# Both attention layers follow an explicit plan of steps

## The chip, the cores and the metric

The kernel runs on one core of a Trainium2 chip. Measured is the device time of one execution in microseconds. Times of the kernel before: 1265.6, 1262.97 and 1261.54 us, median 1262.97.

## The reference

Two transformer layers over T = 512 tokens with D = 1024, in float32:

```
for layer in range(2):
    h = rmsnorm(x, attn_norm[layer])
    if layer == 0:
        fq, fk, fv, ff, dq, ckv, dkr, iq, ik, iw = split(h @ w_in_even)
        fox  = softmax(fq fk' / 8 + c_q - c_k, causal) fv          # 8 heads, c = cumsum(log_sigmoid(ff + b))
        sel  = top_128(sum_h iw_h relu(iq_h ik'), causal)          # per query, 4 index heads
        dsa  = softmax over sel of (dq . [rope key | ckv w_uk]) ; times ckv w_uv   # 8 heads
        x    = x + concat(fox, dsa) @ w_out_even
    else:
        mq, mk, mv = split(h @ w_in_odd)                           # 16 heads, rope on mq and mk
        x    = x + softmax(mq mk' / 8, causal) mv @ w_out_odd
    x = x + conv_glu_ffn(rmsnorm(x, ffn_norm[layer]))
return rmsnorm(x, final_norm)
```

The blocked attention of layer 1 selects one earlier block of 256 keys beside the own block; with 512 tokens these are all keys up to the query, so it is causal attention.

## The kernel before

Everything is held with features on the partitions (xT, 8 tiles of 128 x 512). Each float32 operand is split into a high and a low part, and a product is three matmuls (mm3, L157 to 161). A projection (proj, L163) reads a weight chunk of 128 x 1024: SP loads it into raw_*, ACT copies the high part wh_*, POOL in the attentions of layer 0 (DVE elsewhere) subtracts the low part wl_*. Three buffers each are there for raw, wh and wl, so the SP instruction that loads a chunk waits until the chunk three places earlier has been split. A projection has 24 matmuls of 512 columns; a value group (v_group, L388) has 96 of 256 columns over two chunks and gives the values of two pairs of heads.

The heads are taken in pairs: f0 to f3 and d0 to d3 in layer 0, m0 to m7 in layer 1. A pair's queries are split into h and l and rearranged by three copies of 64 x 512 within SBUF (stack_q, L246: two into the tile a, one into l); its keys by six (stack_k, L255). These moves are issued by SP, on the queue that carries the weights. soft (L332) makes the scores s_* of one head in four blocks of queries on PE, their reductions and masks on DVE (prt_*), the exponentials on ACT, the scaling by POOL. mix (L356) transposes the probabilities on PE (t_*), splits them with ACT and DVE (pt_*, p), and multiplies with the values (o_*). For the d heads a mask tmask comes from index_scores (L608: matmuls ix, then ACT and DVE or POOL) and select (L625), 16 rounds of two DVE instructions for each of three blocks of queries. The values of d come from dv (two PSUM tiles in the pool mm, which has three buffers), split by ACT and DVE.

The program is written in an order that serves as a priority: the framework's scheduler lists the instructions of each engine ahead of time, and each engine then runs its list in order. In the attentions heads() (L527) sets this order: it takes a list of work with due pairs, emits the scores of a head, then a share of the work due by the next pair (the projections of the next pair, selection, output projections), then the mix of the head before. So each pair's keys and queries are projected one pair ahead. In layer 1 the factor 1/rms (rstd_main) and the scaled rope tables are made within the first value group (moba_scale, L741).

Of the kernel before, what the change touches and what calls it, by code (L numbers as in the profile page):

```python
# [71 lines left out]
def hybrid_kernel(ctx: ExitStack, tc: tile.TileContext, xT_d, pos_d, const_d, vec_d, w_d, out_d, idx):  # L72
    nc = tc.nc
    V, A, G, PE = nc.vector, nc.scalar, nc.gpsimd, nc.tensor
# [13 lines left out]
    def tmp(name):  # L88
        return tp.tile([P, T], F32, tag="tmp", name=name, bufs=N_TMP)
# [266 lines left out]
    def mix(nm, e, probs, v, hv, y):  # L356

        par = head_no[0] % 2
        head_no[0] += 1
        rs = (LO, HI)[e]  # L360
        o = ps("O", f"o_{nm}")
        pt = [(big(f"pt_{nm}_{j}h"), big(f"pt_{nm}_{j}l")) for j in range(2)] + [tuple(p3[par])]
        for b in range(3):
            t = ps("T", f"t_{nm}_{b}")
            if b < 2:
                blocks = [(b, i) for i in range(b, NB)]
                segs = [(0, P * len(blocks), 0)]
            else:
                blocks = [(2, 2), (2, 3), (3, 3)]
                segs = [(0, 256, 0), (256, 384, 384)]  # L370
            for n, (j, i) in enumerate(blocks):
                PE.transpose(t[:, n * P:n * P + P], probs[i][:, j * P:j * P + P], ident)  # L372
            ph, pl = pt[b]
            for s0, s1, d0 in segs:
                d1 = d0 + s1 - s0
                split(ph[:, d0:d1], pl[:, d0:d1], t[:, s0:s1])
        for j in range(NB):
            ph, pl = pt[min(j, 2)]
            c0, w, o0 = ((0, T, 0), (0, 384, P), (0, 256, 256), (256, 256, 256))[j]
            vj = v[:, j, hv].rearrange("p s c -> p (s c)")  # L380
            PE.matmul(o[:, o0:o0 + w], vj, ph[:, c0:c0 + w], start=j == 0, stop=False)  # L381
            PE.matmul(o[:, o0:o0 + w], vj, pl[:, c0:c0 + w], start=False, stop=j == NB - 1)
        A.copy(y[rs], o[HI])
        V.tensor_tensor(y[rs], y[rs], o[LO], op=OP.add)
# [139 lines left out]
                done(2 * p + e, Q[1])  # L524
        last(Q[1])

    def heads(pairs, work):  # L527


        work = list(work)  # L530
        prev = None

        def finish(pr):
            p, e, probs = pr
            c = pairs[p]
            mix(f"{c['nm']}{e}", e, probs, values[c["v"]], c["hv"] + e, c["y"])
            if e == 1:
                c["out"].append(halves(c["y"], f"o_{c['nm']}", c.get("lo", V)))

        for p, c in enumerate(pairs):  # L540
            while work and work[0][0] <= p:
# [125 lines left out]
    def fox(p):  # L667
        def vals():
            values["f", p // 2] = v_group(f"fv{p // 2}_")

        def qs():
            c["q"] = stack_q(scaled(proj(f"fq{p}"), f"fq{p}"), f"fq{p}")

        def ks():
            c["k"] = stack_k(scaled(proj(f"fk{p}"), f"fk{p}"), f"fk{p}", G)

        c = {"nm": f"f{p}", "v": ("f", p // 2), "hv": 2 * (p % 2), "bias": causal, "out": fo, "lo": G,
             "decay": [(selr[:, P + h:P + h + 1], ck) for h in (2 * p, 2 * p + 1)]}
        return c, ([vals] if p % 2 == 0 else []) + [ks, qs]

    def dsa(p):
        def vals():
            uh, ul = ukv[0]
            g = p // 2
            vg = vtile(f"dv{g}")
            for b in range(2):
                o = ps("mm", f"mm_dv{g}_{b}", (P, 2, 256))
                for bb in range(2):
                    s = slice((2 * b + bb) * P, (2 * b + bb + 1) * P)
                    ws = slice(512 + 256 * g, 768 + 256 * g)  # L690
# [19 lines left out]
        return c, [ks, qs] + ([vals] if p % 2 == 0 else [])  # L710

    pairs, work = [], []
    for n in range(8):
        c, w = (fox if n < 4 else dsa)(n % 4)
        pairs.append(c)
        if n == 0:
            w = [x for i, f in enumerate(w) for x in (f, lambda i=i: index_scores(i + 1))]
        elif n == 2:
            w.append(lambda: select(1, range(16)))
        elif n > 2 and n < 5:  # L720
            w[1:1] = [lambda n=n: select(n - 1, range(8))]
            w.append(lambda n=n: select(n - 1, range(8, 16)))
        work += [(n, f) for f in w]
        if n == 7:
            work.append((7, lambda: out_proj("oe0_", fo, part=[0])))
    work += [(8, lambda m=m: out_proj("oe0_", fo, part=[m])) for m in range(1, 4)]
    heads(pairs, work)
# [11 lines left out]


    def moba_scale():  # L741
        rstd_main(accs[2], "n2")
        rope_scaled()

    mo = ([], [])

    def moba(p):
        def vals():
            values["m", p // 2] = v_group(f"mv{p // 2}_", moba_scale if p == 0 else None)

# [7 lines left out]
        return c, ([vals] if p % 2 == 0 else []) + [ks, qs]

    pairs, work = [], []  # L760
    for n in range(8):
        c, w = moba(n)
        pairs.append(c)
        work += [(n, f) for f in w]
        if n == 7:
            work.append((7, lambda: out_proj("oo0_", mo[0], part=[0])))
    work += [(8, lambda m=m: out_proj("oo0_", mo[0], part=[m])) for m in range(1, 4)]
    heads(pairs, work)
# [156 lines left out]
```

## Time and profile before

| | |
|---|---|
| median of three runs | 1262.97 us |
| profiled execution | 1261.51 us, span 1259.7 us |
| mean granted clock of TensorE | 0.993 |
| attention of layer 0 (about) | 57 to 290 us of the span |
| attention of layer 1 (about) | 636 to 905 us of the span |

Busy time is the sum of an engine's instructions; matmuls overlap each other in it. A line of the timeline has a start, a busy time, the instruction with output and inputs, and in brackets the idle time ahead of it with what ended it. Granted clock 1.00 is full speed of TensorE.

### The profile page before, as it was taken

How to read it: one execution, taken by the hardware profiler on the slowest of the kernel's cores; microseconds unless marked ns; L12 is line 12 of the kernel's file. 1: busy time of each engine (PE TensorE's matmuls, PEld its weight loads, DVE VectorE, ACT ScalarE, POOL GpSimd, SP SyncE). 2: the span in 40 equal slices, each digit the busy share in tenths (PEclk: the TensorE clock that was granted, in tenths of full speed). 3: DMA queues.
4: the chain of work that ended last, by engine and by line, in shares of the span. 5: the costliest groups of instructions: out<-in, count | busy, mean ns of one | idle time of the engine just before them, and what ended most of it. 6: DMA issues, size and time to landing. Idle time of an engine off the chain costs nothing.

```text
span 1259.7 us, 16807 instructions
## 1 busy us (share of the span) xinstructions
PE 1220.4 (97%) x5996; PEld 1018.3 (81%) x5996; DVE 810.9 (64%) x1489; ACT 557.4 (44%) x969; POOL 357.7 (28%) x394
## 2 busy tenths in 40 slices
PE   6889999999999999999999999999999999999997
PEld 4768778778888888888887888888888888888887
DVE  7889988675654555544666778787655555444555
ACT  5564667653332333333445556555433333332334
POOL 3665557542111111111213223332222111111110
PEclk9989999999999999999999999999999999999999
DMA  5333444222333322323325434331233332333321
GB/s 194 101 92 111 128 99 128 63 80 89 101 100 100 98 90 93 96 93 100 103 96 142 113 100 123 105 109 67 84 93 108 100 100 92 94 100 101 96 88 67
DMA packets 57379, 127.24 MB, mean 101 GB/s; under 512 B 7584, under 2 KB 21024, under 8 KB 57296
## 3 DMA queue, kind: packets, MB, share of 16 engines
q1 hardware_dynamic: 56368, 124.81, 33.2%
q10 hardware_dynamic: 864, 1.17, 0.3%
q8 instruction: 47, 0.77, 0.2%
q14 instruction: 36, 0.29, 0.1%
q0 software_dynamic: 64, 0.20, 0.0%
HBM read 104.13 MB, written 2.10 MB: 84 GB/s over the span
## 4 chain that ended last, share of the span: by engine, by line
PE 79%; DVE 10%; issue 5%; ACT 3%; DMA 2%; POOL 1%; POOLq 0%; ACTq 0%; DVEq 0%; SPq 0%
PE mm_g L160 6%; PE mm_g L161 6%; PE mm_g L159 6%; PE mm_u L161 6%; PE mm_u L159 6%; PE mm_u L160 6%; PE mm_d L161 6%; PE mm_d L160 6%; PE mm_d L159 6%; DVE tmask L630 2%; DVE m L629 1%; DMA mq_l<-mq_h 1%; PE t_m L372 1%; PE o_m L381 1%; PE mm_mk L160 1%
## 5 line engine op out<-in xcount | busy, mean ns | idle before, releaser
L434 POOL TENSOR_TENSOR cv<-cv,gs 128x512 f32<-128x512 f32 x44 | 57.1, 1298 | 546.2 <-ACT gs L433 546.2
L159 PE MATMUL mm_d<-a_h,wh_d 128*128 128x512 f32 (+1 forms) x384 | 142.8, 372 | 0.0
L160 PE MATMUL mm_d<-a_l,wh_d 128*128 128x512 f32 (+1 forms) x384 | 142.6, 371 | 0.0
L161 PE MATMUL mm_d<-a_h,wl_d 128*128 128x512 f32 (+1 forms) x384 | 142.6, 371 | 0.0
L503 DVE TENSOR_TENSOR us<-mm_u,cv 128x512 f32<-128x512 f32 x44 | 30.4, 692 | 168.1 <-PE mm_u L161 132.7
L160 PE MATMUL mm_g<-xl,wh_g 128*128 128x512 f32 x352 | 137.2, 390 | 0.4 <-DVE xl L175 0.4
L159 PE MATMUL mm_u<-xh,wh_u 128*128 128x512 f32 x352 | 137.3, 390 | 0.0
L161 PE MATMUL mm_u<-xh,wl_u 128*128 128x512 f32 x352 | 137.0, 389 | 0.0
L160 PE MATMUL mm_u<-xl,wh_u 128*128 128x512 f32 x352 | 137.0, 389 | 0.0
L161 PE MATMUL mm_g<-xh,wl_g 128*128 128x512 f32 x352 | 137.0, 389 | 0.0
L159 PE MATMUL mm_g<-xh,wh_g 128*128 128x512 f32 x352 | 137.0, 389 | 0.0
L148 ACT CAST wh_g<-raw_g 128x1024 fp32r<-128x1024 f32 x44 | 46.3, 1052 | 143.1 <-PE mm_g L160 141.6
L500 DVE TENSOR_TENSOR gs<-mm_g,RB 128x512 f32<-128x512 f32 x44 | 30.4, 691 | 118.2 <-PE mm_g L161 115.7
L128 ACT CAST wh_d<-raw_d 128x1024 fp32r<-128x1024 f32 x45 | 47.4, 1054 | 123.7 <-PE mm_u L160 103.4
L160 PEld LDWEIGHTS mm_d<-a_l,wh_d 128*128 128x128 f32 x384 | 72.3, 188 | 12.5
L159 PEld LDWEIGHTS mm_d<-a_h,wh_d 128*128 128x128 f32 x384 | 72.3, 188 | 12.5
L161 PEld LDWEIGHTS mm_d<-a_h,wl_d 128*128 128x128 f32 x384 | 72.3, 188 | 12.4
L160 PEld LDWEIGHTS mm_g<-xl,wh_g 128*128 128x128 f32 x352 | 66.1, 188 | 14.8 <-DVE xl L175 1.1
L161 PEld LDWEIGHTS mm_u<-xh,wl_u 128*128 128x128 f32 x352 | 66.1, 188 | 13.8
L159 PEld LDWEIGHTS mm_g<-xh,wh_g 128*128 128x128 f32 x352 | 66.1, 188 | 13.7
L161 PEld LDWEIGHTS mm_g<-xh,wl_g 128*128 128x128 f32 x352 | 66.1, 188 | 13.7
L160 PEld LDWEIGHTS mm_u<-xl,wh_u 128*128 128x128 f32 x352 | 66.1, 188 | 13.6
(778 smaller groups left out, 3072.4 us busy)
## 6 DMA issues: line engine op xcount, KB each, us to landing
raw_g<-in_w SPq DMA_DIRECT2D x44, 512.0 KB, 3.5
raw_u<-in_w SPq DMA_DIRECT2D x44, 512.0 KB, 3.6
raw_d<-in_w SPq DMA_DIRECT2D x41, 256.0 KB, 2.9
raw_d<-in_w SPq DMA_DIRECT2D x29, 192.0 KB, 2.6
raw_d<-in_w SPq DMA_DIRECT2D x34, 128.0 KB, 2.4
raw_oe<-in_w SPq DMA_DIRECT2D x8, 512.0 KB, 4.0
raw_mv<-in_w SPq DMA_DIRECT2D x8, 512.0 KB, 3.5
raw_mk<-in_w SPq DMA_DIRECT2D x8, 512.0 KB, 4.0
```

Of the source, the lines that this page charges most:

```text
L128: A.copy(dst_h, src)
L148: A.copy(wh, raw)
L159: PE.matmul(out, ah, bh, start=first, stop=False)
L160: PE.matmul(out, ah, bl, start=False, stop=False)
L161: PE.matmul(out, al, bh, start=False, stop=last)
L372: PE.transpose(t[:, n * P:n * P + P], probs[i][:, j * P:j * P + P], ident)
L381: PE.matmul(o[:, o0:o0 + w], vj, ph[:, c0:c0 + w], start=j == 0, stop=False)
L434: G.tensor_tensor(cv, cv, gs, op=OP.mult)
L500: V.tensor_tensor(gs, og, RB, op=OP.mult)
L503: V.tensor_tensor(us, ou, cv, op=OP.mult)
L629: V.max(m8, sc)
L630: V.match_replace(sc, m8, sc, -3e38)
```

## The change

heads() goes, and attention() takes its place: it reads a string of steps and emits them as they stand. s is the scores of a head (pair, head), m its mix, k, q and v the projections of a pair (v of a value group), i the index scores of a block, x a quarter of a selection (block, quarter), o a part of the output projection of the finished half. The old order of layer 0 began v0 i1 k0 i2 q0 i3 s00 k1 s01 q1 m00 s10 v2 k2 m01 s11 q2, with all rounds of select(1) behind q2. What a step computes is unchanged; moba_scale is called by whichever projection of layer 1 comes first.

```
+PLAN0 = (
+    "v0 i1 k0 i3 i2 q0 s00 x10 v2 k1 s01 q1 m00 s10 k2 s11 q2 x11 x12 m01 x13 x20 s20 m10 k3 s21 x21 m11 "
+    "x22 x23 x30 q3 s30 m20 k4 x31 q4 s31 v4 x32 x33 m21 m30 s40 k5 m31 s41 q5 m40 s50 k6 q6 m41 s51 q7 "
+    "m50 s60 v6 m51 o0 m60 k7 s61 s70 m61 m70 s71 o1 o2 m71 o3 "
+)
+PLAN1 = (
+    "q1 q0 k0 k1 v0 s00 s01 s10 k2 s11 m00 k3 q4 q2 m01 v2 k4 q3 m10 m11 s20 s21 v4 s30 m20 m21 s31 k5 "
+    "m30 k7 s40 m31 s41 o0 q5 v6 m40 s50 k6 m41 s51 q6 s60 m50 m51 o1 q7 s61 s70 m60 o2 m61 m70 s71 m71 "
+    "o3 "
+)
-    def heads(pairs, work):
...
-            for e in range(2):
-                probs = soft(...)
-                n = len([1 for w in work if w[0] <= p + 1])
-                for _ in range((n + 1 - e) // (2 - e)):
-                    work.pop(0)[1]()
-                if prev is not None:
-                    finish(prev)
-                prev = (p, e, probs)
...
+    def attention(pairs, plan, pieces):
+        probs = {}
+        for step in plan.split():
+            kind, n = step[0], step[1:]
+            if kind == "s":
+                c, e = pairs[int(n[0])], int(n[1])
+                if e == 0:
+                    c["y"] = tmp(f"y_{c['nm']}")
+                probs[n] = soft(...)
+            elif kind == "m":
+                c, e = pairs[int(n[0])], int(n[1])
+                mix(f"{c['nm']}{e}", e, probs.pop(n), values[c["v"]], c["hv"] + e, c["y"])
+                if e == 1:
+                    c["out"].append(halves(c["y"], f"o_{c['nm']}", c.get("lo", V)))
+            else:
+                pieces[kind](int(n))
...
+    attend([fox(p) for p in range(4)] + [dsa(p) for p in range(4)], PLAN0,
+           i=index_scores, x=lambda n: select(n // 10, range(n % 10 * 4, n % 10 * 4 + 4)),
+           o=lambda m: out_proj("oe0_", fo, part=[m]))
...
     def moba_scale():
-        rstd_main(accs[2], "n2")
-        rope_scaled()
+        if 2 in accs:
+            rstd_main(accs.pop(2), "n2")
+            rope_scaled()
...
+        def qs():
+            o = proj(f"mq{p}")
+            moba_scale()
+            c["q"] = stack_q(rope(o, f"mq{p}"), f"mq{p}")
...
+    attend([moba(p) for p in range(8)], PLAN1, o=lambda m: out_proj("oo0_", mo[0], part=[m]))
```

In the listings below, helper lines of the new kernel stand 13 further down; raw_* are weight loads of 512 KB, 64x512 are moves, the numbers in names are buffers'. First, the SP queue around the moves of fq0, ahead of the first scores of layer 0; before:

```order
L147 DMA raw_fk2_1139<-in_w 128x1024
L244 DMA fk0_h_667<-fk0_h_667 64x512
L244 DMA fk0_l_668<-fk0_l_668 64x512
L147 DMA raw_fq2_1262<-in_w 128x1024
L244 DMA fq0_a_747<-fq0_h_743 64x512
L244 DMA fq0_a_747<-fq0_l_744 64x512
L244 DMA fq0_l_744<-fq0_h_743 64x512
L147 DMA raw_fk3_1427<-in_w 128x1024
```

and now:

```order
L160 DMA raw_fk2_1151<-in_w 128x1024
L257 DMA fk0_bh_671<-fk0_h_667 64x512 x2
L257 DMA fk0_bl_675<-fk0_l_668 64x512 x2
L257 DMA fk0_h_667<-fk0_h_667 64x512
L257 DMA fk0_l_668<-fk0_l_668 64x512
L257 DMA fq0_a_775<-fq0_h_771 64x512
L257 DMA fq0_a_775<-fq0_l_772 64x512
L160 DMA raw_fq2_1234<-in_w 128x1024
L257 DMA fq0_l_772<-fq0_h_771 64x512
L160 DMA raw_fk3_1439<-in_w 128x1024
```

The load raw_fq2 stood ahead of the two moves into fq0_a and stands behind them now; raw_fk2 has gone ahead of the moves of fk0.

Second, PE between the value tiles dv0_1 and the query projection dq1 in layer 0; before:

```order
L160 MATMUL mm_dv0_1_1898<-wl_ukv_1717,ckv_h_457 128x256
L161 MATMUL mm_dv0_1_1898<-wh_ukv_1716,ckv_l_458 128x256
L705 MATMUL mm_dk1_2000<-kr_304,selr_85 128x512
L159 MATMUL mm_dk1_2000<-ckv_h_457,wh_ukv_1716 128x512
L160 MATMUL mm_dk1_2000<-ckv_l_458,wh_ukv_1716 128x512
L161 MATMUL mm_dk1_2000<-ckv_h_457,wl_ukv_1717 128x512
L159 MATMUL mm_dq1_2097<-xh_74,wh_dq1_2089 128x512
L160 MATMUL mm_dq1_2097<-xl_75,wh_dq1_2089 128x512
L161 MATMUL mm_dq1_2097<-xh_74,wl_dq1_2090 128x512
```

and now:

```order
L282 MATMUL s_f31_0_1815<-fk3_bl_1483,fq3_l_1648 128x256
L357 MATMUL s_f31_1_1822<-ck_474,selr_85 128x256
L281 MATMUL s_f31_1_1822<-fk3_bh_1479,fq3_l_1648 128x256
L282 MATMUL s_f31_1_1822<-fk3_bl_1483,fq3_l_1648 128x256
L385 MATMUL t_f21_0_1897<-const_70,prt_f21_1488 128x128 x2
L385 MATMUL t_f21_1_1904<-const_70,prt_f21_1488 128x128 x3
L708 MATMUL mm_dk1_2000<-kr_304,selr_85 128x512
L172 MATMUL mm_dk1_2000<-ckv_h_457,wh_ukv_1728 128x512
L173 MATMUL mm_dk1_2000<-ckv_l_458,wh_ukv_1728 128x512
L174 MATMUL mm_dk1_2000<-ckv_h_457,wl_ukv_1729 128x512
L172 MATMUL mm_dq1_2097<-xh_74,wh_dq1_2089 128x512
```

The matmuls of dv0_0 and dv0_1 ended directly ahead of dk1 before; now they are further up (the last of dv0_0 is 34 rows ahead of the first of dq1), and scores of f3 and transposes of f2 stand between.

Third, the SP queue at the end of the attention of layer 0, with the keys dk3 and queries dq3 of the last pair and the weights raw_oe1 of the output projection; before:

```order
L147 DMA raw_oe1_0_2927<-in_w 128x1024
L244 DMA dq2_l_2262<-dq2_h_2261 64x512
L244 DMA dk3_bh_2436<-dk3_h_2432 64x512 x2
L244 DMA dk3_bl_2440<-dk3_l_2433 64x512 x2
L147 DMA raw_oe1_1_2972<-in_w 128x1024
L244 DMA dk3_h_2432<-dk3_h_2432 64x512
L244 DMA dk3_l_2433<-dk3_l_2433 64x512
L244 DMA dq3_a_2488<-dq3_h_2484 64x512
L244 DMA dq3_a_2488<-dq3_l_2485 64x512
L244 DMA dq3_l_2485<-dq3_h_2484 64x512
L147 DMA raw_oe1_2_3019<-in_w 128x1024
```

and now:

```order
L160 DMA raw_oe1_0_2927<-in_w 128x1024
L257 DMA dq3_a_2384<-dq3_h_2380 64x512
L257 DMA dq3_a_2384<-dq3_l_2381 64x512
L257 DMA dq3_l_2381<-dq3_h_2380 64x512
L160 DMA raw_oe1_1_2972<-in_w 128x1024
L160 DMA raw_oe1_2_3019<-in_w 128x1024
L257 DMA dk3_bh_2597<-dk3_h_2593 64x512 x2
L257 DMA dk3_bl_2601<-dk3_l_2594 64x512 x2
L257 DMA dk3_h_2593<-dk3_h_2593 64x512
L257 DMA dk3_l_2594<-dk3_l_2594 64x512
L160 DMA raw_oe1_3_3066<-in_w 128x1024
```

The moves of dk3 have gone behind raw_oe1_2 and behind the moves of dq3.

Fourth, the SP queue at the start of layer 1, with the moves of the first queries and keys; before:

```order
L147 DMA raw_mk2_6270<-in_w 128x1024
L244 DMA mk0_bh_5873<-mk0_h_5869 64x512 x2
L244 DMA mk0_bl_5877<-mk0_l_5870 64x512 x2
L244 DMA mk0_h_5869<-mk0_h_5869 64x512
L147 DMA raw_mq2_6390<-in_w 128x1024
L244 DMA mk0_l_5870<-mk0_l_5870 64x512
L244 DMA mq0_a_5922<-mq0_h_5918 64x512
L244 DMA mq0_a_5922<-mq0_l_5919 64x512
L147 DMA raw_mk3_6503<-in_w 128x1024
L244 DMA mq0_l_5919<-mq0_h_5918 64x512
L244 DMA mk1_bh_5999<-mk1_h_5995 64x512 x2
```

and now:

```order
L160 DMA raw_mv0_0_5904<-in_w 128x1024
L160 DMA raw_mv0_1_5958<-in_w 128x1024
L160 DMA raw_mk2_6115<-in_w 128x1024
L257 DMA mq1_a_5754<-mq1_h_5750 64x512
L257 DMA mq1_a_5754<-mq1_l_5751 64x512
L160 DMA raw_mk3_6231<-in_w 128x1024
L257 DMA mq1_l_5751<-mq1_h_5750 64x512
L257 DMA mq0_a_5799<-mq0_h_5795 64x512
L257 DMA mq0_a_5799<-mq0_l_5796 64x512
L257 DMA mk0_bh_5844<-mk0_h_5840 64x512 x2
L257 DMA mk0_bl_5848<-mk0_l_5841 64x512
L257 DMA mq0_l_5796<-mq0_h_5795 64x512
```

The queries mq1 and mq0 are projected first now, and all their moves stand ahead of the keys' second moves; the scores of pair 0 come behind the keys of both pairs and the value group mv0 on PE.

## Rows read from the trace of the kernel before

**Rows 1.** Page, part 1: busy time, share of the span and instructions of each engine.
```profile
PE 1220.4 (97%) x5996; PEld 1018.3 (81%) x5996; DVE 810.9 (64%) x1489; ACT 557.4 (44%) x969; POOL 357.7 (28%) x394
```

**Rows 2.** Windows: start:end length, busy us by engine, granted clock, DMA share, GB/s.
```profile
57.00:100.00 43.00, 37.38 (x171) 30.16 (x171) 36.68 (x100) 27.46 (x55) 30.96 (x38) 0.92 0.36 106
83.87:90.70 6.83, 6.13 (x19) 5.36 (x20) 3.71 (x14) 3.79 (x10) 1.89 (x3) 0.50 0.09 22
100.00:150.00 50.00, 48.22 (x284) 41.21 (x284) 47.96 (x125) 24.13 (x55) 26.68 (x38) 1.00 0.37 103
169.20:172.60 3.40, 3.40 (x9) 2.63 (x8) 3.25 (x7) 0.31 (x1) 1.85 (x3) 0.50 0.16 18
290.00:636.00 346.00, 346.00 (x1529) 286.58 (x1528) 185.85 (x226) 118.94 (x145) 65.70 (x49) 1.00 0.31 97
636.00:800.00 164.00, 158.16 (x961) 138.15 (x960) 119.11 (x265) 86.58 (x193) 45.14 (x57) 1.00 0.41 112
```

**Rows 3.** Waits of PE, 57 to 290 us: total us, times, longest.
```profile
PE s_f L268 <- DMA fq_a<-fq_l: 3.3, 1, 3.3
...
PE t_f L372 <- DVE pt_f_0l L129: 1.9, 4, 1.3
PE mm_dq L159 <- DVE dv L129: 1.8, 1, 1.8
```

**Rows 4.** Waits of PE, 636 to 905 us (layer 1).
```profile
PE s_m L268 <- DMA mq_l<-mq_h: 3.3, 3, 1.3
PE s_m L268 <- DMA mq_a<-mq_l: 1.0, 1, 1.0
```

**Rows 5.** Timeline, PE before the first scores: start, us, instruction, [idle before <-releaser].
```profile
80.88 0.40 PE L161 MATMUL mm_fk<-xh,wl_fk 128*128 128x512 f32 x1
84.57 0.58 PE L268 MATMUL s_f<-fk_h,fq_a 128*128 128x256 f32 x1 [3.29 <-DMA fq_a<-fq_l]
```

**Rows 6.** Timeline, SP queue, the same stretch (DMA issues).
```profile
79.24 0.33 SPq L147 DMA_DIRECT2D raw_fq<-in_w  x1
79.62 0.46 SPq L244 DMA_DIRECT2D fq_a<-fq_h  x1
```

**Rows 7.** Waits of SP, 60 to 90 us.
```profile
SPq L147 <- POOL wl_fv L152: 4.1, 1, 4.1
```

**Rows 8.** Tile fq_a: issue to landing of its moves.
```profile
DMA to landing us min/median/max: 4.4/4.5/4.5
```

**Rows 9.** Tile mq_a, layer 1: issue to landing.
```profile
DMA to landing us min/median/max: 2.2/2.2/4.6
```

**Rows 10.** Tile mq_l, layer 1: issue to landing.
```profile
DMA to landing us min/median/max: 2.2/2.6/5.2
```

**Rows 11.** Timeline, PE around mm_dq.
```profile
164.35 0.28 PE L159 MATMUL mm_dv<-wh_ukv,ckv_h 128*128 128x256 f32 x1
...
165.67 0.28 PE L161 MATMUL mm_dv<-wh_ukv,ckv_l 128*128 128x256 f32 x1
...
166.26 0.39 PE L160 MATMUL mm_dk<-ckv_l,wh_ukv 128*128 128x512 f32 x1
166.49 0.40 PE L161 MATMUL mm_dk<-ckv_h,wl_ukv 128*128 128x512 f32 x1
168.65 0.50 PE L159 MATMUL mm_dq<-xh,wh_dq 128*128 128x512 f32 x1 [1.77 <-DVE dv L129]
```

**Rows 12.** Timeline, DVE around the copy of dv.
```profile
166.80 1.19 DVE L228 TENSOR_TENSOR ry_dq<-ry_dq,rs_dq 128x512 f32<-128x512 f32 x1 [1.30 <-POOL rs_dq L227]
167.92 0.68 DVE L129 TENSOR_TENSOR dv<-mm_dv,dv 128x512 fp32r<-128x512 f32 x1
```

**Rows 13.** Timeline, PE at the first scores of layer 1.
```profile
670.67 0.36 PE L268 MATMUL s_m<-mk_h,mq_a 128*128 128x256 f32 x1 [0.98 <-DMA mq_a<-mq_l]
```

**Rows 14.** Timeline, SP queue there.
```profile
669.55 0.33 SPq L147 DMA_DIRECT2D raw_mk<-in_w  x1
670.55 0.46 SPq L244 DMA_DIRECT2D mq_l<-mq_h  x1
```

More of the change, by code (lines that the diff above doesn't have):

```diff
@@ L525, in ffn @@
         last(Q[1])
-    def heads(pairs, work):
[L530 to L541, printed above, removed]
-                work.pop(0)[1]()
-            c["y"] = tmp(f"y_{c['nm']}")
-            for e in range(2):
-                probs = soft(f"{c['nm']}{e}", e, c["q"], c["k"], c["bias"], c["decay"][e] if "decay" in c else None)
-                n = len([1 for w in work if w[0] <= p + 1])
-                for _ in range((n + 1 - e) // (2 - e)):
-                    work.pop(0)[1]()
-                if prev is not None:
-                    finish(prev)
-                prev = (p, e, probs)
-        finish(prev)
-        for w in work:
-            w[1]()
+    def attention(pairs, plan, pieces):
[6 more added lines that the diff above has]
+                    c["y"] = tmp(f"y_{c['nm']}")
+                probs[n] = soft(f"{c['nm']}{e}", e, c["q"], c["k"], c["bias"], c["decay"][e] if "decay" in c else None)
+            elif kind == "m":
[5 more added lines that the diff above has]
+                pieces[kind](int(n))
     values = {}
@@ L678, in fox @@
              "decay": [(selr[:, P + h:P + h + 1], ck) for h in (2 * p, 2 * p + 1)]}
-        return c, ([vals] if p % 2 == 0 else []) + [ks, qs]
+        return c, ks, qs, vals
     def dsa(p):
@@ L709, in dsa, with attend @@
         c = {"nm": f"d{p}", "v": ("d", p // 2), "hv": 2 * (p % 2), "bias": [causal[0]] + tmask[1:], "out": do}
[L710 to L727, printed above, removed]
+        return c, ks, qs, vals
+    def attend(made, plan, **pieces):
+        for k, n in (("k", 1), ("q", 2), ("v", 3)):
+            pieces[k] = lambda p, n=n: made[p][n]()
+        attention([m[0] for m in made], plan, pieces)
+    attend([fox(p) for p in range(4)] + [dsa(p) for p in range(4)], PLAN0,
+           i=index_scores, x=lambda n: select(n // 10, range(n % 10 * 4, n % 10 * 4 + 4)),
+           o=lambda m: out_proj("oe0_", fo, part=[m]))
     acc = sq_acc(1)
@@ L748, in vals @@
         def vals():
-            values["m", p // 2] = v_group(f"mv{p // 2}_", moba_scale if p == 0 else None)
+            values["m", p // 2] = v_group(f"mv{p // 2}_", moba_scale)
         def qs():
-            c["q"] = stack_q(rope(proj(f"mq{p}"), f"mq{p}"), f"mq{p}")
+            o = proj(f"mq{p}")
+            moba_scale()
+            c["q"] = stack_q(rope(o, f"mq{p}"), f"mq{p}")
         def ks():
-            c["k"] = stack_k(rope(proj(f"mk{p}"), f"mk{p}"), f"mk{p}")
+            o = proj(f"mk{p}")
+            moba_scale()
+            c["k"] = stack_k(rope(o, f"mk{p}"), f"mk{p}")
         c = {"nm": f"m{p}", "v": ("m", p // 2), "hv": 2 * (p % 2), "bias": causal, "out": mo[p // 4]}
[L758 to L768, printed above, removed]
+        return c, ks, qs, vals
+    attend([moba(p) for p in range(8)], PLAN1, o=lambda m: out_proj("oo0_", mo[0], part=[m]))
     accs[3] = sq_acc(3)
```

## Prediction

> **What bounds the kernel now.** The page's line of engines comes first: PE is busy 97% of the span [rows 1], so TensorE is the bound and the other engines matter where PE waits for them. The windows tell where it does. In the feed-forward network of layer 0 (290 to 636 us) PE is busy 346.00 of 346 us at full clock; between 57 and 100 us it is busy 37.38 of 43 us at a granted clock of 0.92, and between 636 and 800 us 158.16 of 164 us [rows 2]. So only the attentions have anything to give. The lists of waits name it [rows 3, 4]. In layer 0: the first scores s_f for the DMA into fq_a (3.3 us), transposes t_f for a DVE copy (1.9 in four), mm_dq for a DVE copy of dv (1.8). In layer 1: s_m for mq_l (3.3 in three) and for mq_a (1.0). Each end is seen at one instruction: s_f at 84.57 after 3.29 idle [rows 5], mm_dq at 168.65 after 1.77 [rows 11], s_m at 670.67 after 0.98 [rows 13]. The profile counts idle time from the modelled end of the matmul before, 0.40 after its start; matmuls of 512 columns follow each other at 0.23 (166.26 to 166.49 [rows 11]), so by pitch each such gap is 0.16 longer: from 80.88 + 0.23 to 84.57 are 3.46 us [rows 5], and mm_dq lost 1.93.
>
> Two of the waits cost more than their idle time. From 83.87 to 90.70 the granted clock is 0.50, the lower of the two levels (1.2 of 2.4 GHz), behind the 3.29 us; 90.70 - 84.57 = 6.13 us ran there at half speed, which is 3.0 us lost. Behind the 1.77 us at mm_dq the window from 169.20 to 172.60 shows 0.50 too: 3.40 / 2 = 1.7 us lost. Layer 1, with its four shorter waits, shows 1.00 from 636 to 800 [rows 2].
>
> **First scores of layer 0: +5.7 us.** SP issued the weight raw_fq at 79.24 and right behind it, from 79.62, the two moves into fq_a [rows 6]; SP had stood 4.1 us for that weight's buffer, which POOL frees [rows 7]. These two landed 4.4 to 4.5 us after issue, where a move takes 2.2 at its fastest (mq_a, minimum and median) [rows 8, 9]. The new order puts that weight (raw_fq2) behind both moves. PE also gets some more to do between the end of the projection fq0 and the first scores: 45 matmuls of 256 columns of fv1, against 18 of 512 columns of fk1. At 0.12 us each (11 steps from 164.35 to 165.67 [rows 11]) and 0.23 that is 5.4 against 4.1 us. Against this, two blocks of index scores now stand before the end of fq0, which hang on ACT, and the copies fq_h and fq_l queue on ACT and DVE behind theirs. My estimate is that fq_a is issued by 79.8 and lands at about 82.1, where PE is through at about 81.4: a wait of 0.75, shorter than those of layer 1, which left the clock alone. Gain 3.46 - 0.75 = 2.7, and 3.0 from the clock: 5.7. Bounds: 4.0 if the wait is as long as 2.4, without half clock; 6.5 if there is none.
>
> **Transposes in layer 0: +1.5 us.** DVE is busy 47.96 of 50 us between 100 and 150 [rows 2], most of it with the selection rounds, and PE waited 1.9 us for its copies there [rows 3]. In the new order selection comes in quarters (x10, x11, ...) behind the copies of each head. Counting PE and DVE work in the order up to each transpose, DVE stands about 3 us less far behind PE than before. I take 1.5; bounds 0 and 1.9.
>
> **dv before mm_dq: +3.6 us.** mm_dq1 needs the PSUM tile of dv0_0. Before, 1.6 us of PE work lay between dv0_0's last matmul and mm_dq1, and the DVE copy of dv at 167.92 stood behind the add of ry_dq at 166.80, which waited 1.30 for POOL [rows 12]. Now scores of f3 and transposes of f2 lie between: 19 matmuls of 256 columns, 3 of 384, 7 of 512 and 7 transposes, 19 x 0.12 + 3 x 0.18 + 7 x 0.23 + 7 x 0.08 = 5.0 us. That is longer than the 3.6 us that the copy took here (from dv0_0's last matmul, about 165.0, to 168.65), so the whole of it goes: 1.93 and 1.7 from the clock. Bounds 0 and 3.6.
>
> **First scores of layer 1: +4.9 us.** Four waits for mq_a and mq_l, 3.3 + 1.0 in the list [rows 4], by pitch 4 x 0.16 more: 4.9. The pattern is that of [rows 6]: raw_mk is issued at 669.55 and the move into mq_l at 670.55, which lands 5.2 us later (the slowest) [rows 10, 14]. In the new order the moves of m0 have 22 us of PE work between projection and scores (8.9 before) for mq_a and 25 (12.3) for mq_l; mq2_l has 34 and mq4_l 71 (14 before). Even a move behind a weight (5.2) hides in that. Bounds 3.9 and 4.9.
>
> **What the new order costs.** Three places. (1) End of layer 0: the key projection dk3 stands late. Its moves on SP stand behind raw_oe1_1 and raw_oe1_2; its cast on ACT stands behind copies of d2; and from the end of mm_dk3 to the first scores s_d30 there are 12.7 us of PE work (20.5 before), of which about 7 behind the transposes that hold the cast. The chain is cast 0.6, four issues 2.2, first moves 2.2 to 4.4, second moves 2.2: 7 to 9.5 us. From the last scores to the transposes of d30 are 3.1 us of PE work (16 before), to those of d31 4.3 (8 before). I take 1.2 + 0.7 + 0.6 = 2.5; bounds 0.5 and 5. (2) Layer 1: the first scores come at once behind v0, whose copies stand on DVE before their reductions (0.8); mq6_a has 9.8 us (10.4 before), mq7_a 6.8 (11.6), so 1.2 and 0.3: 2.3 together, bounds 0 and 4.5. (3) The second FOX pair: fq1_l has 9.6 us of cover instead of 21.4 with a weight ahead of it: 0.4, bounds 0 and 0.5. The norm of layer 1, which PE waits for once (bc), now has 18 matmuls of 512 columns over it, 4.1 us, where it had 33 of 256, 3.9: nothing changes. The number of matmuls stays, and the feed-forward networks and the start stay as they are.
>
> **Sum.** Against the profiled execution: 1261.5 - 5.7 - 1.5 - 3.6 - 4.9 + 2.5 + 2.3 + 0.4 = 1251.0 us. The median of the runs shown is 1.5 above that execution, so 1252.5.
>
> **The Trainium skill against this change.** The rows of moves show 2.2 us at the least and 4.4 to 5.2 behind a weight [rows 8 to 10]. DMA: Bandwidth & Descriptors (the Trainium skill), section Queues, rings and completion order, says that SP's copies share one ring on each of the same DMA engines and that descriptors are consumed there in ring order. By that rule what counts is what stands ahead on SP, and the new order has put two weights ahead of dk3's moves: the end of layer 0 would go as in rival B, 1256.3 instead of the sum. The trace agrees on the size of such a delay; whether PE still has other work by then it cannot show.
>
> **Rivals.** (B) The ends take it back. The moves of dk3 and of mq6/mq7 stand behind 512 KB weights, and each costs what the first scores cost before: 3.3 idle and 3.0 clock, 6.3. In place of the 2.5 at dk3 alone: 1252.5 + 3.8 = 1256.3; in place of the 1.5 at mq6/mq7 as well, 4.8 more: 1261.1. For it: [rows 8 to 10], and that the cover is shorter at both. Against: the cover is still 7 to 12 us at each. (C) Slower: DVE is the bound from 57 to 165 us. It has only 2.04 us free between 100 and 150 [rows 2], the selection (16 rounds for each of three blocks of queries) is not shortened, and fv1's 11.3 us of PE work (96 x 0.118), which covered it, now stand earlier. Then PE, early by 5.7, waits again at the transposes: gains of 5.7, 1.5 and 3.6 go, and two more waits long enough for the half clock, 3.0 and 1.7, come: 1263.0 - 4.9 + 5.2 + 4.7 = 1268.0. It decides once PE waits over 7 us for DVE copies in that stretch (1.9 before). Against: DVE had 6.3 us free between 57 and 100 [rows 2], and the lag in the order falls. (D) The first scores stay as late: raw_fk2 now stands ahead of fk0's moves, waits for POOL as raw_fq did and holds the whole queue. Then 5.7 go: 1258.2. For it: SP stood 4.1 us for such a buffer [rows 7]. Against: that buffer comes free earlier in the new order than the moves' own data.
>
> **How the numbers follow.** A measurement here can tell about 0.3%, 3.8 us: faster is below 1259.2, slower above 1266.8. Forecast 0.67, B 0.15, C 0.08, D 0.10. The forecast's own bounds: all gains high and all costs low, 6.5 + 1.9 + 3.6 + 4.9 - 0.5 = 16.4, gives 1246.6; the bad ends give 4.0 + 3.9 - 10.0 = -2.1, that is 1265.1, not likely together. The range, 1247 to 1262, holds the forecast but for its last tenth, B and D. Faster: 0.65 of the forecast, 0.03 of B, 0.08 of D = 0.76. Same: 0.02, 0.12, 0.02 = 0.16. Slower: C = 0.08.
>
> **What would show it.** Right: s_f of f0 waits under 1 us, no half clock between 80 and 92; no wait of mm_dq for dv; no wait of s_m for mq in the first half of layer 1; waits of s_d and t_d at dk3 of about 2.5 together. Wrong: a wait of over 2 us with a half clock at s_d30 or at m6 (B); many waits of t_f and t_d for DVE before 170 us (C); s_f for fq_a still about 3 us (D).

## The result and the profile after

The median of four runs is 1248.43 us, against 1262.74 us of the kernel before in four runs beside them: a ratio of 0.9878 (95% interval 0.9860 to 0.9897), 14.3 us less. The forecast was 1252.5, in a range from 1247 to 1262. The profiled execution took 1246.87 us (span 1245.1).

The page's engine line and the windows that answer [rows 1, 2], columns as there:

```profile
PE 1212.8 (97%) x5996; PEld 1011.9 (81%) x5996; DVE 810.3 (65%) x1489; ACT 555.9 (45%) x969; POOL 358.2 (29%) x394
```

```profile
57.00:100.00 43.00, 38.84 (x224) 33.08 (x224) 40.77 (x118) 27.40 (x55) 32.01 (x38) 1.00 0.39 108
80.00:92.00 12.00, 10.45 (x75) 9.58 (x74) 11.62 (x39) 5.72 (x14) 9.19 (x14) 1.00 0.41 111
100.00:150.00 50.00, 48.39 (x254) 39.80 (x253) 46.85 (x124) 26.04 (x63) 27.61 (x40) 1.00 0.45 112
165.00:175.00 10.00, 10.00 (x60) 8.61 (x59) 7.02 (x24) 8.64 (x24) 5.38 (x9) 1.00 0.20 44
...
632.00:790.00 158.00, 157.64 (x967) 138.10 (x966) 121.71 (x264) 82.91 (x184) 42.53 (x53) 1.00 0.45 124
```

The granted clock is 1.00 in all of them: the half clocks of 83.87 to 90.70 and 169.20 to 172.60 are gone. From 632 to 790 us PE is busy 157.64 of 158 us, where it had been 158.16 of 164 [rows 2]. DVE is as busy as before between 100 and 150 us (46.85 of 50), and PE's waits for it in layer 0's attention add up to 2.0 us (0.8, 0.8 and 0.4 below) instead of 3.7 (1.9 and 1.8 in [rows 3]).

What PE still waits for in layer 0's attention, and in layer 1's (the lists answer [rows 3, 4]):

```profile
PE ix L281 <- ACT rl L621: 2.3, 1, 2.3
PE s_f L281 <- DMA fq_a<-fq_l: 2.2, 2, 1.2
PE s_f L357 <- DVE mx_f L361: 0.8, 2, 0.5
PE t_d L385 <- DVE pt_d_0l L142: 0.8, 1, 0.8
PE t_f L385 <- DVE pt_f_0l L142: 0.4, 1, 0.4
```

```profile
PE bc_n L217 <- DVE y_n L214: 0.4, 1, 0.4
```

The wait for fq_a is down from 3.3 in one to 2.2 in two; mm_dq does not stand in the list any more; of the waits of s_m none is left. The SP queue shows the first of these (it answers [rows 6]):

```profile
77.83 0.46 SPq L257 DMA_DIRECT2D fq_a<-fq_h  x1
79.08 0.46 SPq L257 DMA_DIRECT2D fq_a<-fq_l  x1
83.70 0.33 SPq L160 DMA_DIRECT2D raw_fq<-in_w  x1
84.08 0.46 SPq L257 DMA_DIRECT2D fq_l<-fq_h  x1
```

The two moves into fq_a went at 77.83 and 79.08, without a weight ahead; raw_fq came 4.6 us later, at 83.70.

Where the 14.6 us between the two profiled executions lie is read from the three places where PE broadcasts a norm (bc_n): behind the attention of layer 0, ahead of that of layer 1, and behind it. The trace of after, then that of before:

```profile
279.00 0.62 PE L217 MATMUL bc_n<-const,y_n 128*128 128x128 f32 x4 [0.18 <-DVE y_n L214]
...
639.52 0.62 PE L217 MATMUL bc_n<-const,y_n 128*128 128x128 f32 x4 [0.36 <-DVE y_n L214]
...
880.64 0.62 PE L217 MATMUL bc_n<-const,y_n 128*128 128x128 f32 x4
```

```profile
287.10 0.62 PE L204 MATMUL bc_n<-const,y_n 128*128 128x128 f32 x4 [0.15 <-DVE y_n L201]
...
647.56 0.62 PE L204 MATMUL bc_n<-const,y_n 128*128 128x128 f32 x4 [0.61 <-DVE y_n L201]
...
896.28 0.62 PE L204 MATMUL bc_n<-const,y_n 128*128 128x128 f32 x4 [0.17 <-DVE y_n L201]
```

Up to the first one the new kernel is 287.10 - 279.00 = 8.1 us ahead (0.8 of it from before 64 us, where both run the same list). From the first to the second both take 360.5 us: the feed-forward network is untouched. From the second to the third the attention of layer 1 takes 241.1 instead of 248.7: 7.6 us. The stretch behind took 1.0 us longer in this execution (364.5 against 363.4, the same instructions).

### The profile page after: what moved, and what is told of

It is laid out like the page before. It is cut to its first block, busy times and chain, and to the rows that moved or that the text cites. A ratio compares the mean times of both kernels' runs of the same rounds, so it can differ in the third digit from the quotient of the medians.

```text
span 1245.1 us, 16811 instructions
## 1 busy us (share of the span) xinstructions
PE 1212.8 (97%) x5996; PEld 1011.9 (81%) x5996; DVE 810.3 (65%) x1489; ACT 555.9 (45%) x969; POOL 358.2 (29%) x394
## 4 chain that ended last, share of the span: by engine, by line
PE 77%; issue 3%; DVE 2%; POOL 1%; ACT 0%; POOLq 0%; DVEq 0%; ACTq 0%
PE mm_g L173 6%; PE mm_g L172 6%; PE mm_g L174 6%; PE mm_u L173 6%; PE mm_u L174 6%; PE mm_u L172 6%; PE mm_d L173 6%; PE mm_d L172 6%; PE mm_d L174 6%; PE t_m L385 1%; PE mm_mk L174 1%; PE mm_mk L172 1%; PE mm_mk L173 1%; PE mm_mq L174 1%; PE mm_mq L172 1%
## 5 line engine op out<-in xcount | busy, mean ns | idle before, releaser
L173 PEld LDWEIGHTS mm_g<-xl,wh_g 128*128 128x128 f32 x352 | 66.1, 188 | 14.3 <-DVE xl L188 0.6
L172 PEld LDWEIGHTS mm_u<-xh,wh_u 128*128 128x128 f32 x352 | 66.1, 188 | 13.6
L174 PEld LDWEIGHTS mm_g<-xh,wl_g 128*128 128x128 f32 x352 | 66.1, 188 | 13.6
```

The source lines that it names most:

```text
L172: PE.matmul(out, ah, bh, start=first, stop=False)
L173: PE.matmul(out, ah, bl, start=False, stop=False)
L174: PE.matmul(out, al, bh, start=False, stop=last)
```

## The experiments

Since the plan is a string, each experiment is an edit of it. The old orders written as plans give the instruction lists of the kernel before (in the traces of l1_only and q_act every engine runs the same sequence as in that of before up to the end of layer 0's attention), so a part can be undone alone. Each ratio is to runs of the kernel before taken beside that experiment, whose medians were 1260.8 to 1262.7 us; the first row gives those beside after. The last two columns are PE's lost time: the sum, over all matmuls from 57 to 290 us and from 620 to 905 us of the profiled execution, of what lies between two starts beyond the usual pitch of that shape, which is its median step (waits and half clock together; shorter steps count against).

| kernel | median us | ratio to before (95% interval) | lost, layer 0 | lost, layer 1 |
|---|---|---|---|---|
| before | 1262.74 | 1 | 25.4 | 14.0 |
| after | 1248.43 | 0.9878 (0.9860 to 0.9897) | 18.4 | 6.9 |
| l0_only | 1254.87 | 0.9955 (0.9940 to 0.9970) | 19.2 | 13.4 |
| l1_only | 1252.57 | 0.9937 (0.9919 to 0.9955) | 23.4 | 6.9 |
| i_old | 1272.51 | 1.0102 (1.0075 to 1.0128) | 43.4 | 6.6 |
| v2_back | 1258.30 | 0.9978 (0.9966 to 0.9990) | 28.0 | 7.0 |
| w_pool | 1254.60 | 0.9942 (0.9921 to 0.9963) | 19.9 | 7.0 |
| i_old_w_pool | 1263.81 | 1.0020 (1.0003 to 1.0036) | 28.5 | 6.4 |
| q_act | 1270.87 | 1.0079 (1.0056 to 1.0102) | 27.1 | 24.6 |
| start_new | 1253.04 | 0.9932 (0.9915 to 0.9948) | 18.3 | 12.1 |
| q0_i | 1264.38 | 1.0031 (1.0017 to 1.0045) | 34.6 | 6.4 |
| k7_early | 1250.53 | 0.9913 (0.9892 to 0.9935) | 21.1 | 6.9 |
| s20_late2 | 1248.41 | 0.9896 (0.9873 to 0.9918) | 19.8 | 7.2 |
| q2_first | 1256.32 | 0.9956 (0.9940 to 0.9972) | 25.5 | 7.1 |

In four cases the lost time accounts for the medians: i_old loses 25.0 us more than after in layer 0 and is 24.1 slower, q0_i 16.2 and 16.0, v2_back 9.6 and 9.9, start_new 5.2 in layer 1 and 4.6. It holds less well elsewhere: w_pool loses 1.6 more and is 6.2 slower, because its start is later, and s20_late2 loses 1.7 more and is as fast. Part of such a difference is chance: behind the wait of 2.3 us at ix, which all kernels but q0_i have, the profiled execution of l0_only, i_old_w_pool, q_act, s20_late2 and q2_first ran at half clock for a while and the others did not, which is 1.1 to 1.4 us of their lost time.

### The two layers apart

l0_only has the new PLAN0 and the old order of layer 1, l1_only the other way round:

```
-PLAN1 = "q1 q0 k0 k1 v0 s00 s01 s10 k2 s11 m00 k3 q4 ..."        (l0_only)
+PLAN1 = "v0 k0 q0 s00 k1 s01 q1 m00 s10 v2 k2 m01 s11 q2 ..."
-PLAN0 = "v0 i1 k0 i3 i2 q0 s00 x10 v2 k1 s01 q1 m00 ..."         (l1_only)
+PLAN0 = "v0 i1 k0 i2 q0 i3 s00 k1 s01 q1 m00 s10 v2 ..."
```

> The new plan in layer 0, the old order in layer 1. If the two attentions don't act on each other, this takes layer 0's part alone: the rate of the two traces says 7.2 us between the start and the end of that attention, so about 1255.5 us, with the waits of s_m for mq_a and mq_l back as they were (about 4.9 us by pitch). The split of the prediction (7.9 in layer 0 net, 2.6 in layer 1 net) would give 1254.8, which this run alone can't tell from it; l1_only can.

> The old order in layer 0, the new plan in layer 1. By the two traces layer 1 gained 7.6 us: about 1255.1. By the prediction's split, in which first scores behind v0, mq6 and mq7 cost 2.3, it gains 2.6: about 1260.1. The half clock at 84 and at 169 us should be back in both.

Measured: 0.45% and 0.63% faster, of 1262 us that is 5.7 and 8.0 us; together 13.6, near the 14.3 to 15.4 of both. As far as these medians can tell, the layers don't act on each other, and layer 1 gains what the two traces say, not the 2.6 of the prediction. PE's list of waits in layer 1 of l0_only has four waits of s_m again, three for mq_l and one that now ends with ACT's mk_h instead of mq_a:

```profile
PE s_m L281 <- DMA mq_l<-mq_h: 2.3, 3, 1.0
PE s_m L281 <- ACT mk_h L141: 1.1, 1, 1.1
PE o_m L394 <- ACT pt_m_0h L141: 0.7, 4, 0.2
```

In l1_only the first stall of layer 0 (3.1 us) is back with its half clock (0.91 from 80 to 100 us). The wait of mm_dq is back too, 1.8 us, but the clock behind it stays at 1.00 there:

```profile
150.00:175.00 25.00, 22.09 (x122) 17.81 (x121) 22.09 (x56) 15.89 (x39) 10.99 (x15) 1.00 0.44 111
```

The same list of instructions gave 0.50 from 169.20 to 172.60 in the profiled execution of before, and 0.66 from 171 to 176 in that of q_act; so that half clock does not come in every execution.

### What the first scores hang on

```
-    "v0 i1 k0 i3 i2 q0 s00 x10 v2 k1 s01 q1 m00 s10 k2 ..."
+    "v0 i1 k0 i2 q0 i3 s00 x10 v2 k1 s01 q1 m00 s10 k2 ..."     (i_old)
+    "v0 i1 k0 i3 i2 q0 s00 x10 k1 s01 q1 m00 s10 v2 k2 ..."     (v2_back)
```

> The new plan, but the index scores of layer 0 in their old place (i1 k0 i2 q0 i3 instead of i1 k0 i3 i2 q0). That alone puts the weight load raw_fq2 ahead of the moves into fq0_a on the SP queue again, while the matmuls of fv1 still stand between fq0 and the first scores. Theory 1 (the place on the queue decides the first stall): the moves land 4.4 us after issue again, s_f waits about 2 us or more (3.3 less the 1.2 that fv1 covers more), the granted clock falls to 0.5 behind it if the wait is long enough; 1251 to 1254 us. Theory 2 (the value group as cover decides): the wait stays about 1 us, 1248.5.

> The new plan, but the second value group back behind s10. raw_fq2 stays behind the moves into fq0_a, and fk1 instead of fv1 stands between fq0 and the first scores. Theory 1 (place on the queue): the moves land 2.2 to 2.5 us after issue, the wait grows from 1.0 by the 1.2 to 1.4 us of cover that is lost, to about 2.2; 1249.6 without half clock, about 1252 with it. Theory 2 (cover): the first stall is back as before, 3.3 us and half clock, 1254.

Both went further than either theory. In i_old the first stall is back as theory 1 has it: raw_fq waits for its buffer and goes ahead of the moves into fq_a, and s_f waits 3.07 us although fv1 stands in front:

```profile
79.51 0.33 SPq L160 DMA_DIRECT2D raw_fq<-in_w  x1
79.90 0.46 SPq L257 DMA_DIRECT2D fq_a<-fq_h  x1
```

```profile
84.68 0.58 PE L281 MATMUL s_f<-fk_h,fq_a 128*128 128x256 f32 x1 [3.07 <-DMA fq_a<-fq_l]
```

But the exchange of two index blocks costs 24 us against the new kernel, and PE's list of waits says why:

```profile
PE s_f L281 <- DMA fq_a<-fq_l: 5.2, 2, 3.1
PE s_d L281 <- DMA dq_l<-dq_h: 4.4, 1, 4.4
PE s_f L281 <- DMA fq_l<-fq_h: 4.1, 1, 4.1
...
PE s_d L282 <- DMA dk_l<-dk_l: 2.3, 1, 2.3
```

Four more moves are late: PE waits for them at 118, 172, 212 and 256 us, the last some 180 us behind the edit. The longest wait, for dq_l, stands so on SP and on PE:

```profile
201.71 0.46 SPq L257 DMA_DIRECT2D dq_a<-dq_l  x1
206.88 0.33 SPq L160 DMA_DIRECT2D raw_oe<-in_w  x1
207.27 0.46 SPq L257 DMA_DIRECT2D dq_l<-dq_h  x1
```

```profile
207.31 0.40 PE L174 MATMUL mm_dq<-xh,wl_dq 128*128 128x512 f32 x1
212.10 0.55 PE L281 MATMUL s_d<-dk_bh,dq_l 128*128 128x256 f32 x1 [4.40 <-DMA dq_l<-dq_h]
```

The move into dq_l could go when those into dq_a had landed (issued up to 201.71, 2.2 us at best: 204). But raw_oe0_3 stood ahead of it and waited 4.6 us, in SP's list of waits, for POOL's wl_oe; it went at 206.88, and the move behind it landed 4.8 us later. In the new kernel's list raw_oe0_3 stands behind dq1_l and most moves of the next pair's keys (189.02, dq_l at 186.51). The edit of the index blocks has moved the place of the loads on SP all through the layer.

The cover on PE is not what differs: counted in the instruction order, dq1_l has 18.7 us of PE work in i_old and 16.9 in the new kernel. The buffer that raw_oe0_3 needs is freed by wl_oe0_0, and that hangs on the move's own pair: ACT makes dq1_h and behind it, in its list, the cast wh_oe0_0, and POOL follows:

```profile
200.34 0.62 ACT L141 CAST dq_h<-ry_dq 128x512 fp32r<-128x512 f32 x1
200.87 1.06 ACT L161 CAST wh_oe<-raw_oe 128x1024 fp32r<-128x1024 f32 x1
```

```profile
204.04 2.81 POOL L165 TENSOR_TENSOR wl_oe<-raw_oe,wh_oe 128x256 fp32r<-128x256 f32 x4
```

So from dq1_h to the load are 6.5 us (200.34 to 206.88), and the move goes after it. In the new kernel the same way is 6.3 us long (182.74 to 189.02), but the move does not stand behind it. That an earlier projection would not help follows from these lists; no run tests it.

v2_back shows the other half. The first scores wait only 0.72 us, less than in the new kernel, so the value group isn't what hides that; it hides the second head's move (6.6 us in two waits for fq_l here, none in the new kernel):

```profile
81.59 0.36 PE L281 MATMUL s_f<-fk_h,fq_a 128*128 128x256 f32 x1 [0.72 <-DMA fq_a<-fq_l]
...
89.33 0.36 PE L281 MATMUL s_f<-fk_bh,fq_l 128*128 128x256 f32 x1 [3.58 <-DMA fq_l<-fq_h]
```

The move into fq_l can go only when both moves into fq_a have landed, and raw_fq is between them (at 83.88, the move at 84.27), as it is in the new kernel (83.70 and 84.08). With fv1 in front it has 18.8 us of PE work as cover, without it 8.8.

### Weights on another queue

```
-        nc.sync.dma_start(raw, w_d[idx[name]])
+        (G if lo_on_pool else nc.sync).dma_start(raw, w_d[idx[name]])     (w_pool; i_old_w_pool with i_old's plan)
```

> The order of i_old (index scores in their old place, 1272.5 us there), with the weight loads of layer 0's attention issued by POOL. In i_old six waits of s_f and s_d end with a move that stands behind a weight on SP: 3.1, 2.1, 4.1, 4.4, 2.3 us idle, with half clocks behind some. Theory 1 (queue of SP): nearly all go, 1250 to 1254 us. Theory 2 (the order on PE itself, or the shared DMA engines): the waits stay, 1268 or above.

> The new plan, with the weight loads of layer 0's attention issued by POOL instead of SP. Theory 1 (on SP a weight that waits for its buffer, and then its 512 KB, hold back the moves behind it): the moves land 2.2 to 2.6 us after issue, the two waits of s_f for fq_a (1.2 + 1.3 us) go, about 1246 us, less what POOL loses by issuing 24 loads. Theory 2 (the transfers share the DMA engines whatever the queue): landings of 4 to 5 us stay, and the time is 1248 or above.

With the plan of i_old the lost time in layer 0 falls from 43.4 to 28.5 us: the waits for dq_l (4.4) and dk_l (2.3) are gone, that for fq_l is 0.7 instead of 4.1, and the first stall is 1.9 instead of 3.1. So the place on SP's queue was behind these. Landings stay long all the same, as theory 2 has it: moves of dk_h still take up to 4.9 us. What is left of the waits:

```profile
PE t_d L385 <- POOL prt_d L366: 3.0, 4, 1.3
PE s_f L281 <- DMA fq_a<-fq_l: 2.8, 3, 1.9
...
PE t_f L385 <- DVE pt_f_0l L142: 2.2, 2, 2.0
...
PE mm_dq L172 <- DVE dv L142: 1.0, 1, 1.0
```

The time falls by less than the lost time, by 8.7 us, because the start is later: the index scores that wait for ACT come at 69.12 instead of 64.33 us. With the new plan it is the same (67.46 instead of 63.22), and nothing is won: the wait at f2 goes, the first one grows from 1.0 to 1.8 us, and mm_dq waits for dv again (1.6). The loads themselves are not late there: the fifth of them goes at 41.83 us, where it goes at 41.55 in the new kernel. One subtraction on DVE is long, and PE waits behind it; in w_pool:

```profile
42.70 4.80 DVE L142 TENSOR_TENSOR iq_l<-ry_iq,iq_h 128x512 fp32r<-128x512 f32 x1
```

```profile
49.48 1.11 PE L205 MATMUL st_kv<-const,sqkv 128*128 128x128 f32 x4 [4.49 <-ACT sqkv L639]
```

In the new kernel that subtraction takes 1.10 us (at 42.69) and the wait is 0.76. Beside the long one POOL works without a gap from 42.42 to 46.95 us; whether that is what holds DVE up is not shown.

```
-        move(a[LO], h[LO])
+        eng = nc.scalar if nm[0] == "m" else nc.sync
+        move(a[LO], h[LO], eng)       # and the two others
```

> The old order in both layers, with the three moves of the queries of layer 1 issued by ACT instead of SP; the weights stay on SP. Theory 1 (queue of SP): mq_a and mq_l land in 2.2 to 2.6 us, and the four waits of s_m (4.9 us by pitch) go: about 1258, less what ACT loses by 24 issues. Theory 2 (shared DMA engines): slowest landings stay at 4.6 to 5.2 us, time as before, 1261 to 1263.

This failed as a remedy. PE waits 7.5 us for mq_a in layer 1 instead of 1.0 (five times), and ACT's list has waits of its own for the moves:

```profile
ACT p L141 <- DMA mq_a<-mq_l: 7.5, 2, 4.1
```

ACT's cast of the probabilities stood 7.5 us, in two waits, behind a move that waited for the one before. And the landings did not become short: mq_l has minimum, median and maximum

```profile
DMA to landing us min/median/max: 2.2/3.7/5.2
```

though no weight shares ACT's queue. Theory 2 holds for the transfer, theory 1 for the issue; ACT as the issuer has a wait of its own.

### Layer 1: start or cover

```
-    "q1 q0 k0 k1 v0 s00 s01 s10 k2 s11 m00 k3 q4 q2 m01 v2 k4 q3 ..."
+    "q1 q0 k0 k1 v0 s00 s01 s10 m00 v2 k2 m01 s11 q2 m10 s20 k3 m11 s21 q3 ..."
```

> The new plan in layer 0; in layer 1 only the start of the new plan (both queries and keys of pairs 0 and 1 ahead of v0, then s00 s01 s10), and from there the old order. If cover for each pair's moves is what counts, the two waits of pair 0 (2.7 us by pitch) stay gone, and those of m2 and m4 for mq_l (2.3) and the small waits of o_m for ACT (1.4) come back: 1248.4 + 3.7 = 1252. If the start alone is the gain: 1248.5.

Measured 1253.04. Pair 0 waits no more; the later waits are back:

```profile
PE s_m L281 <- DMA mq_l<-mq_h: 1.4, 1, 1.4
PE s_m L281 <- DVE sm_m L364: 1.0, 1, 1.0
PE o_m L394 <- ACT pt_m_0h L141: 0.8, 4, 0.2
```

The two waits of s_m stand at m2 and m4 (712 and 763 us), at matmuls that read mq_l; the profile puts the second down to DVE. So about 3 of the 7.6 us come from the start and over 4 from the later pairs: these two waits, whose queries the plan projects early, and the four of o_m.

### Four tries to better the new plan

```
-"v0 i1 k0 i3 i2 q0 s00"              +"v0 k0 i1 i3 i2 q0 s00"                (q0_i)
-"s60 v6 m51 o0 m60 k7 s61"           +"s60 k7 v6 m51 o0 m60 s61"             (k7_early)
-"x13 x20 s20 m10 k3 s21"             +"x13 m10 k3 x20 s20 s21"               (s20_late2)
-"k2 s11 q2"                          +"q2 s11 k2"                            (q2_first)
```

> The new plan with the first key projection ahead of the first index scores (v0 k0 i1 i3 i2 q0 instead of v0 i1 k0 i3 i2 q0). In both kernels PE waits 2.3 us at 63 us for ACT, which copies the values and the cumulated decay ahead of the first relu. Eight more matmuls of fk0 (1.8 us) then stand ahead of that place, so the wait should shrink to about 0.5; raw_fq2 stays behind the moves into fq0_a. If PE's gain is kept at the first scores: about 1246.5. Rival: fq_a then lands as late as before, and PE waits the 1.8 us there instead (1.0 becomes up to 2.8, with half clock): 1248 to 1251.

> The new plan with the last key projection of layer 0 two steps earlier (s60 k7 v6 m51 o0 m60 s61 instead of s60 v6 m51 o0 m60 k7 s61). The prediction put 2.5 us of cost on the late dk3; the trace of the new kernel shows no wait of s_d30 at all and about 1.4 us of small waits of t_d for POOL there. If it was those that the late place costs: 1247 to 1248; if the place is worth nothing: 1248.5.

> The new plan with the scores of f2 later (x13 m10 k3 x20 s20 s21 instead of x13 x20 s20 m10 k3 s21). In the new kernel s_f of f2 waits 1.2 us at 130 us for the move into fq_a, which stands behind raw_dq1 on SP. The cover between the projection fq2 and these scores grows from 7.9 to 9.4 us: the wait should go, 1247.2. Rival: the transposes of f20, nearer behind their scores now (5.3 instead of 7.2 us), wait for DVE or POOL instead: 1248.5 or above.

> The new plan with query and key projection of f2 exchanged (q2 s11 k2 instead of k2 s11 q2). The move into fq_a of f2, for which PE waits 1.2 us in the new kernel, gets 14.6 instead of 7.9 us of PE work as cover; raw_dq1 still stands ahead of it on SP. Theory 1 (cover): the wait goes, 1247.2. Theory 2 (what stands ahead on SP waits for its buffer, however long the cover): a wait of s_f stays, for fq_a or for the key's moves, which come last now with 8.4 us of cover: 1248.5 or above.

q0_i took away the wait aimed at (ix, 2.3 us, is gone from the list, with 1.2 of mm_fq in its place) and lost 16 us: at the first scores 2.3, as the rival had it, and then, as in i_old, at moves that the new list puts behind raw_oe:

```profile
PE s_d L281 <- DMA dq_l<-dq_h: 4.4, 1, 4.4
PE s_d L282 <- DMA dk_l<-dk_l: 2.4, 1, 2.4
PE s_f L281 <- DMA fq_a<-fq_l: 2.3, 1, 2.3
```

k7_early shows that the late dk3 costs nothing that an earlier one would save: the small waits of t_d went, and the output projection waits 2.7 us for a DVE copy of dv instead (median 1250.53, not to be told from the new kernel's). s20_late2 took away the wait of f2 for fq_a, and mm_dq waits 1.3 us for dv in its place: 1248.41, the same. q2_first gave fq_a of f2 the cover it lacked, and the key's move came behind raw_dq (130.61, the move at 131.70):

```profile
135.29 0.50 PE L281 MATMUL s_f<-fk_h,fq_a 128*128 128x256 f32 x2 [3.12 <-DMA fk_h<-fk_h]
```

with a half clock behind it (0.94 from 120 to 150 us), and 2.1 us for fq_l; theory 2. None of the four beats the new plan.

## Why the prediction was right, and where it was not

As a whole the forecast fell 4 us short, and that is nearly all layer 1: the sum held 7.9 us for layer 0, where the traces show 7.3 (8.1 less the 0.8 from before), and 2.6 for layer 1, where they show 7.6. Within layer 0 the terms were off both ways and partly cancelled, which was luck.

**First scores, +5.7.** Right, and somewhat too much: PE's lost time from 80 to 93 us fell from 6.5 to 1.9, by 4.5. The gap is 1.02 us instead of 3.29, and no half clock follows. The reason is the one given, the place of raw_fq2 on SP: i_old puts that back, by exchanging two index blocks, and has the gap again (3.07). The cover by fv1, which the prediction added, does not matter there, as v2_back shows; it matters for fq_l, which the prediction did not look at.

**Transposes, +1.5.** Right for the transposes of the f heads: waits of t_f for DVE 0.4 instead of 1.9. But the gain was not kept, which the sum did not foresee: s_f waits 0.8 for DVE's mx_f and t_d 0.8 for pt_d, neither of which stands in the list of before.

**dv, +3.6.** The wait is gone (1.9 by pitch). The 1.7 of half clock was in the profiled execution of before, but l1_only, with the same list, has the wait without it; as a gain of the median 3.6 was too much by a part of that. The margin is thin: in w_pool and s20_late2 the wait is there again (1.6 and 1.3), with these instructions in the order of the new kernel or nearly so.

**First scores of layer 1, +4.9.** Right: none of the four waits is left, and l0_only brings four back.

**Costs, -5.2.** This is the step that failed, by its second part most. Layer 1 was to lose 2.3: no wait of s_m for mq6, mq7 or behind v0 stands in the list. It gained 1.3 more at o_m, which had waited four times for ACT's pt_m_0h (they are there in l0_only and start_new), and 1.4 at the transposes t_m, and the sum held neither; so layer 1 came to 7.6 where 2.6 were forecast. For the end of layer 0 the 2.5 were too much and wrong in place: s_d30 never waits, since the moves of dk3 had landed (the last by 227.8 us) ahead of the scores that read them (the last move's from 229.15 on), and PE had other work until then. But PE lost 2.9 us more than before, by pitch, at transposes of d: 0.9 at 204.88 for DVE, ahead of dk3, and some 1.5 from 222 to 236 us in pieces of 0.35 and less, most for POOL's prt_d. The second FOX pair was to lose 0.4; it was f2 that waited 1.2, behind raw_dq.

**Rival B** did not come. raw_oe1_2 had gone by 218.1 us, the moves of dk3 went from 220.37 to 225.56, and landed in 2.2 to 3.5 us. The Trainium skill, DMA: Bandwidth & Descriptors, section Queues, rings and completion order, read as in the prediction, would have made the end of layer 0 go as in rival B, 1256.3. The queries' moves that ACT issued in q_act took up to 5.2 us, as on SP's queue. The Trainium skill, DMA: Bandwidth & Descriptors, section Issuing engines are not separate DMA queues, says that transfers that different engines start run on the same DMA engines and interleave, so a second issuer saves only the issue; the trace of q_act agrees.

**Rivals C and D** did not come either. DVE holds PE for 0.4 us at t_f and 0.8 at s_f, not for the 7 of rival C. For rival D, raw_fk2 did go ahead of fk0's moves, at 69.65, but the moves into fq_a went at 77.83 all the same. A time above that of before, as C forecast, did come for a plan of the same kind, by SP and not by DVE: i_old, one exchange away, is 0.8 to 1.3% slower than the kernel before.

## What to carry to other kernels

Where weights and small copies share one queue, look for each copy at what stands ahead of it: a load that waits for a buffer holds everything behind it (4.6 us for raw_oe0_3 in i_old). If that buffer is freed by work that stands behind the copy's own source, work put in between on the busy engine should be no cover; this is argued from the lists of i_old, not tested alone. When a scheduler decides the order, an edit in one place can move loads a hundred microseconds further on, so compare the whole queue before and after, not the edited place. And value a plan as a whole: in the four tries here a single wait that was taken out of this order came back elsewhere.

## What the runs showed of the hardware

A wait of 1.8 us on PE ahead of mm_dq was followed by 3.4 us at the lower clock in one execution and by none in another of the same instruction list (before: 0.50 from 169.20 to 172.60; l1_only: 1.00 from 150 to 175), while the wait of 3.1 to 3.3 us at the first scores had it both times. The wait of 2.33 us at ix was followed by the lower clock in 5 of the 13 profiled executions that have it: from 57 to 80 us the granted clock is 0.93 in l0_only, i_old_w_pool, q_act, s20_late2 and q2_first and 1.00 in the rest, before among them; so the length of a wait alone does not decide it. A move of 64 x 512 issued by ACT landed as late as 5.2 us behind weights that SP had issued, no better than from SP. And with the 25 weight loads of layer 0 issued by POOL a subtraction of 128 x 512 on DVE took 4.80 us instead of 1.10, in both kernels that do so (w_pool, i_old_w_pool), and the index scores behind it came 4.2 and 4.8 us later.
